# A two-layer encoder on one Trainium2 core: where the second group's FFN norm keeps its values, and which engine makes the operands of the feed-forward products

## The chip, the core and the metric

The kernel runs on one core of a Trainium2 chip. The core has a matmul engine (TensorE, PE in the profile; PEld is its weight load), three elementwise engines (VectorE or DVE, ScalarE or ACT, GpSimd or POOL) and a queue engine for transfers (SyncE, SP). ScalarE's queue issues transfers too. The metric is the time on the device of one execution, in microseconds (us); the median of three runs of the kernel before is 2719.42 us (2717.59 to 2723.7).

## The reference, cut to what matters

Two request groups ("prompt" and "sample", 512 tokens each) go through two layers with shared weights. Per layer, with `mod` a shift, scale and gate per group and channel:

```
h = rms_norm(x, norm_attn_g) * (1 + scale_a) + shift_a
x = x + gate_a * (mixers(h @ w_in) @ w_out)
h = rms_norm(x, norm_ffn_g) * (1 + scale_f) + shift_f
u = h @ w_up                                    # 1024 -> 2 x 2816
u = conv3(u, conv_w) + conv_b                   # 3 taps along the tokens, per channel
val, gate = split(u)
x = x + gate_f * ((val * silu(gate)) @ w_down)  # 2816 -> 1024
```

All of it is float32. The change touches the second half: the FFN norm, the up-projection and the down-projection.

## The kernel before

**Products in halves.** A float32 operand is used as a pair: a high half `hi` (rounded by ScalarE) and a low half `lo = value - hi`, made by an elementwise engine ("split"). One product of a 128x128 weight block with a 128x512 activation block takes three matmuls (`mm3`, L172 to L174). Tiles named `whi`, `wlo` are halves of weights, `hh`, `hl` of activations, `th`, `tl` of sums of activations. A weight split goes into a ring of 768 columns (`w_split`), so a 512-column split is one instruction or two of 256.

**Up-projection.** The 22 blocks `f` of the up-projection each have a value and a gate half. For the first `n1` = 2 blocks the four quarter products (two groups x two halves of the 1024 input channels) are computed plainly (`plain_up`, eight accumulators in all, 24 matmuls each). For the other 20 blocks seven products replace eight (the Strassen-Winograd scheme): weight blocks and activation blocks are first added and subtracted, `w_combos` for the weights, T1 to T4 for the activations, where B11, B21 are the two channel halves of group 0 and B12, B22 those of group 1. T1 = B12 - B11, T2 = B22 - T1, T3 = B22 - B12, T4 = B21 - T2, on whole values, each split again. Before, the whole values of both groups are not kept: `whole` adds `hh` and `hl` back together each time (L1091), `minus` forms the differences and the low halves (L1094). Each product of the seven (`mm7`) is 12 matmuls.

**What stands around it.** After the products of a block, ScalarE and DVE run the conv (`conv3`, L1160, L1161, L1163): ScalarE's instruction and two on DVE read the PSUM bank, so the bank is free only when L1163 is done. `glu` applies silu on ScalarE, multiplies (L1169) and stores the gate product through ScalarE's queue (L1170). The PSUM pools `p_mm`, `p_sc` and `p_tp` have two banks each. In the first layer 63 pieces of the modulation product for the second layer (`ada_cols`, L242, `csx`) are placed between the products; `ag` places eight of them after the first and the second product of block 2.

**FFN norm.** `outproj` forms the residual of a group, `norm_rstd` its per-token scale, `norm_rows` spreads the scale over the partitions with four transposes (L282), `norm_apply` scales (L296), shifts and splits. For odd channel blocks POOL makes the low half (L304), for even ones DVE (L307).

**Down-projection.** The 22 blocks are taken in groups of pairs (`gr`: 3, 3, 3 pairs and four plain blocks in layer 0; 4, 3, 4 pairs in layer 1). Per pair there are four weight sums (`w_combos`) and four activation sums (`g_combos`), seven products with a split on either side, and the results are added into the residual from PSUM (`add_x`, L1313): 28 additions per group.

**Who does what, and in which order.** Letters in the table `P` choose the engine of each elementwise step in turn ('p' POOL, 'v' DVE; 'vvp' is two of three on DVE): `uf` the first weights' splits, `tb`/`tl` the activation sums and their splits, `ug` the gate product, `us`/`ul` the later weights' sums and splits, `ds`, `db`, `dl` the down-projection's sums and splits (`d0`, `d1`, `d2` for its first group). A scheduler with a timeline of its own sets each engine's order; each engine then works its list strictly in order. `issue_after` adds an ordering between two instructions.

## Time and profile before

| | us |
|---|---|
| median of three runs | 2719.42 |
| profiled execution: device time | 2725.8 |
| profiled execution: span | 2724.0 |
| PE / DVE / ACT / POOL busy in it | 2562.2 / 2018.2 / 1410.9 / 1143.0 |

| stage | from - to | length | PE busy | DVE | POOL | clock |
|---|---|---|---|---|---|---|
| modulation, attention, output projections, layer 0 | 0 - 693.6 | 693.6 | 639.9 | 461.9 | 220.4 | 0.98 |
| plain products, layer 0 | 693.6 - 738.9 | 45.3 | 45.3 | 38.8 | 26.3 | 1.00 |
| first later products, layer 0 | 738.9 - 780.1 | 41.2 | 16.7 | 41.2 | 28.8 | 0.71 |
| other later products, layer 0 | 780.1 - 1194.3 | 414.2 | 411.4 | 302.7 | 157.4 | 1.00 |
| down-projection in pairs, layer 0 | 1194.3 - 1382.8 | 188.5 | 175.8 | 183.5 | 138.0 | 0.97 |
| rest of layer 0, attention of layer 1 | 1382.8 - 2025.2 | 642.4 | 618.8 | 408.5 | 220.4 | 0.98 |
| plain products, layer 1 | 2025.2 - 2069.7 | 44.5 | 44.5 | 38.5 | 25.3 | 1.00 |
| first later products, layer 1 | 2069.7 - 2108.6 | 38.9 | 15.9 | 38.9 | 28.4 | 0.65 |
| other later products, layer 1 | 2108.6 - 2485.1 | 376.5 | 376.4 | 300.8 | 153.2 | 1.00 |
| down-projection, layer 1 | 2485.1 - 2720.3 | 235.2 | 217.6 | 202.7 | 145.0 | 0.97 |

The page gives each engine's busy time, its course over 40 slices, and the granted clock of PE as a share of full speed. A matmul's record (0.39 us) is longer than the step to the next one, because matmuls are pipelined; the step is what counts. Idle time of PE is attributed to whatever released it: "DVE t L1163" is a conv step on DVE. A busy engine is not necessarily working at its best price, since an instruction's record also covers the time in which it is held up.

### The profile page before, as it was taken

What the parts mean: (1) busy time and instruction counts of PE and PEld (TensorE: products, weight loads), DVE (VectorE), ACT (ScalarE), POOL (GpSimd) and SP (SyncE); (2) the same over time, 40 slices, a digit from 0 to 9 for tenths busy, and PEclk for the clock granted to TensorE, in tenths of its full rate; (3) what the DMA queues carried; (4) which work ended last, traced back from release to release, by engine and by line L of the source; (5) the groups of instructions that cost most, each with busy time, mean ns of one, the idle gap of its engine ahead of it and who ended that gap; (6) DMA issues with size and microseconds to landing.
All of it is one profiled execution on the core that took longest, in us unless ns stands there. A gap on an engine that the chain in (4) does not pass through costs nothing. (4 is left out here: it accounts for less than half of the span.)

```text
span 2724.0 us, 39807 instructions
## 1 busy us (share of the span) xinstructions
PE 2562.2 (94%) x13836; PEld 2160.4 (79%) x13836; DVE 2018.2 (74%) x3639; ACT 1410.9 (52%) x3058; POOL 1143.0 (42%) x811
## 2 busy tenths in 40 slices
PE   8899999999879999998999999999996999999988
PEld 4788889888657777776788989898875888887767
DVE  6677577665887777789964765867469878878986
ACT  4466566564444445453444756756544555555422
POOL 2321212256644433428853122122667344441884
PEclk9999999999989999999999999999997999999999
DMA  7743545565144444452224345445651222224321
GB/s 265 217 116 107 130 109 141 145 188 181 66 163 144 142 140 128 151 205 101 93 76 113 86 114 136 113 118 148 191 181 47 86 78 87 76 86 185 109 85 62
DMA packets 146433, 347.69 MB, mean 128 GB/s; under 512 B 21372, under 2 KB 27260, under 8 KB 144952
## 3 DMA queue, kind: packets, MB, share of 16 engines
q1 hardware_dynamic: 133560, 322.08, 39.1%
q10 hardware_dynamic: 12672, 23.07, 2.3%
q8 instruction: 109, 1.79, 0.3%
q14 instruction: 92, 0.75, 0.1%
HBM read 241.19 MB, written 59.51 MB: 110 GB/s over the span
## 5 line engine op out<-in xcount | busy, mean ns | idle before, releaser
L162 POOL TENSOR_TENSOR wlo<-s,whi 128x768 fp32r<-128x768 f32 (+1 forms) x131 | 237.3, 1820 | 429.3 <-ACT whi L160 406.2
L172 PE MATMUL ps_mm<-hh,whi 128*128 128x512 f32 x932 | 369.7, 399 | 35.5 <-DVE t L1163 26.2
L173 PE MATMUL ps_mm<-hl,whi 128*128 128x512 f32 x932 | 369.0, 396 | 5.0 <-DVE hl L1094 3.7
L174 PE MATMUL ps_mm<-hh,wlo 128*128 128x512 f32 x932 | 367.5, 394 | 6.3 <-POOL wlo L1094 3.5
L172 PE MATMUL ps_mm<-whi,hh 128*128 128x256 f32 (+1 forms) x1104 | 342.0, 311 | 9.7 <-ACT raw L533 6.7
L173 PE MATMUL ps_mm<-wlo,hh 128*128 128x256 f32 (+1 forms) x1104 | 338.1, 307 | 1.3 <-POOL wlo L162 1.3
L174 PE MATMUL ps_mm<-whi,hl 128*128 128x256 f32 (+1 forms) x1104 | 337.9, 307 | 0.0
L1094 DVE TENSOR_TENSOR wlo<-fr,whi 128x512 fp32r<-128x512 f32 (+1 forms) x385 | 304.0, 807 | 38.2 <-ACT whi L1098 30.3
L1169 POOL TENSOR_TENSOR t<-t 128x512 f32<-128x512 f32 x88 | 127.9, 1453 | 428.0 <-issue 111.3
L1098 ACT ACTIVATE whi<-fr 128x512 fp32r<-128x512 f32 (+1 forms) x416 | 199.6, 517 | 176.3 <-PE ps_mm L173 65.5
L172 PEld LDWEIGHTS ps_mm<-hh,whi 128*128 128x128 f32 x932 | 176.2, 190 | 83.4 <-issue 22.0
L172 PEld LDWEIGHTS ps_mm<-whi,hh 128*128 128x128 f32 x1104 | 214.0, 194 | 13.4 <-ACT raw L533 7.5
L173 PEld LDWEIGHTS ps_mm<-wlo,hh 128*128 128x128 f32 x1104 | 214.3, 194 | 4.2 <-POOL wlo L162 2.2
L174 PEld LDWEIGHTS ps_mm<-whi,hl 128*128 128x128 f32 x1104 | 213.6, 194 | 1.5
L174 PEld LDWEIGHTS ps_mm<-hh,wlo 128*128 128x128 f32 x932 | 176.8, 190 | 44.1 <-POOL wlo L1094 3.9
L173 PEld LDWEIGHTS ps_mm<-hl,whi 128*128 128x128 f32 x932 | 177.0, 190 | 42.5 <-DVE hl L1094 5.4
L160 ACT ACTIVATE whi<-s 128x768 fp32r<-128x768 f32 (+1 forms) x153 | 123.6, 815 | 129.9 <-DMA s<-in_w_in 32.4
L641 DVE CUSTOM_DVE_ANT_0 S<-ps_sc,bias 128x512 f32<-128x512 f32 (+3 forms) x288 | 150.2, 529 | 53.5 <-PE ps_sc L677 41.1
L1161 DVE SCALAR_TENSOR_TENSOR t<-u,cw,t 128x511 f32<-128x511 f32 x120 | 118.1, 984 | 63.4 <-ACT t L1160 62.6
L636 DVE TENSOR_TENSOR ptl<-ps_tp,pth 128x256 fp32r<-128x256 f32 (+1 forms) x240 | 129.7, 552 | 47.8 <-ACT pth L635 46.2
L1160 ACT ACTIVATE t<-u,cw 128x512 f32<-128x512 f32 x120 | 97.6, 813 | 122.8 <-DVE u L1091 107.1
L172 PE MATMUL ps_sc<-hh,whi 128*128 128x512 f32 x404 | 159.1, 395 | 1.1 <-DVE x L1313 1.1
(351 smaller groups left out, 6934.2 us busy)
## 6 DMA issues: line engine op xcount, KB each, us to landing
fr<-in_w_up SPq DMA_DIRECT2D x88, 512.0 KB, 3.8
sa<-in_w_adac SPq DMA_DIRECT2D x56, 512.0 KB, 5.9
s<-in_w_in SPq DMA_DIRECT2D x64, 384.0 KB, 3.6
g_sp<-t ACTq DMA_DIRECT2D x88, 256.0 KB, 4.1
stk<-pr_h SPq DMA_DIRECT2D x152, 128.0 KB, 2.3
stk<-pr_l SPq DMA_DIRECT2D x152, 128.0 KB, 2.4
s<-in_w_ada SPq DMA_DIRECT2D x50, 384.0 KB, 3.3
s<-in_w_out SPq DMA_DIRECT2D x40, 384.0 KB, 3.2
```

The lines of the kernel that those rows point to most:

```text
L160: nc.scalar.activation(hi[:, :cols], s[:, :cols], AF.Copy)
L162: self.eng[self.count % len(self.eng)].tensor_tensor(lo[:, :cols], s[:, :cols], hi[:, :cols].bitcast(F32), op=ALU.subtract)
L172: nc.tensor.matmul(out_, a[0], b[0], start=start, stop=False, skip_group_check=True)
L173: nc.tensor.matmul(out_, a[0], b[1], start=False, stop=False, skip_group_check=True)
L174: return nc.tensor.matmul(out_, a[1], b[0], start=False, stop=stop, skip_group_check=True).ins
L636: nc.vector.tensor_tensor(lo[:, :n], pt[:, :n], hi[:, :n].bitcast(F32), op=ALU.subtract)
L641: nc.vector.tensor_tensor_reduce(s[:, :n], p, b, 1.0, init, op0=ALU.add, op1=ALU.min, accum_out=mn)
L1094: pick(key).tensor_tensor(o, a, b, op=ALU.subtract)
L1098: nc.scalar.activation(hi, s, AF.Copy)
L1160: nc.scalar.activation(t, p, AF.Identity, scale=c4[:, 1:2], bias=c4[:, 3:4])
L1161: nc.vector.scalar_tensor_tensor(t[:, 1:], p[:, :T - 1], c4[:, 0:1], t[:, 1:], op0=ALU.mult, op1=ALU.add)
L1169: pick('ug').tensor_tensor(a, a, b, op=ALU.mult)
```

## The change

- **Second group's norm.** `outproj` hands over the residual and the scale of group 1; the scaling, shift and split now stand in the up-projection, between the first and the second plain block of group 0. The scaled and shifted value stays whole in `xk` (first four channel blocks) and `vk`, and is split by ScalarE (high) and DVE (low). T1, T2, T3 are formed in place from the whole values, and `whole` is gone. `plain_up` takes an instruction after which its later accumulators and conv steps are issued (`x_last`, the last scaling).
- **Group 0's norm and the attention norm.** The odd-block branch with POOL is gone: ScalarE writes the high half, DVE the low half, for all blocks.
- **Engines.** A key 'ut' (= 'v') replaces 'tb', 'tl' and 'uf', and serves for the gate products of the plain blocks and the weight sums of block 2. 'ds', 'db', 'dl' become 'v' for all groups of the down-projection.
- **Modulation.** 'ag' is gone; all 63 pieces are spread from block 3.2 to block 21.2.
- **Memory.** The pool with the attention's S and residual tiles moves to the right-hand side and stays open until group 0's plain products; T1, T2 and most of T4 then take its place.

```diff
-P = {..., 'ds': 'p', 'db': 'p', 'dl': 'vvp', 'd2': 'v', ..., 'd0': 'v', 'd1': 'v', ..., 'ag': [[4, 4, 0], []]}
+P = {..., 'ds': 'v', 'db': 'v', 'dl': 'v', ..., 'ut': 'v'}
...
-                if k % 2:
-                    nc.scalar.activation(t, t, AF.Identity, bias=sh)
-                    nc.scalar.activation(hi, t, AF.Copy)
-                    norm_last[0] = nc.gpsimd.tensor_tensor(lo, t, hi.bitcast(F32), op=ALU.subtract).ins
-                else:
-                    nc.scalar.activation(hi, t, AF.Identity, bias=sh)
-                    norm_last[1] = nc.vector.scalar_tensor_tensor(lo, t, sh, hi.bitcast(F32), ...).ins
+                nc.scalar.activation(hi, t, AF.Identity, bias=sh)
+                nc.vector.scalar_tensor_tensor(lo, t, sh, hi.bitcast(F32), op0=ALU.add, op1=ALU.subtract)
...
-                    hf.append(norm_apply(s_tile, xo, norm_rows(r), l, 1, g))
+                    if g == 0:
+                        hf.append(norm_apply(s_tile, xo, norm_rows(r), l, 1, g))
+                    else:
+                        hf.append((xo, r))
...
-                    pick('ug').tensor_tensor(a, a, b, op=ALU.mult)
+                    pick('ug' if f >= NC1 else 'ut').tensor_tensor(a, a, b, op=ALU.mult)
...
-                ada_at = [NC1 + (2.5 + i) / 7 for i, n in enumerate(n_gap) for _ in range(n)]
-                rest = 9 * len(mine) - len(ada_at)
+                rest = 9 * len(mine)
...
-                    plain_up(0)
-                    with tc.issue_after(norm_last[0]), tc.issue_after(norm_last[1]):
-                        for k in range(4):
-                            u = us[k]
-                            t = ft("t")
-                            whole(t, B12[k])
-                            minus('tb', u, t, u)
-                            split('tl', u, T1[k])
...
-                    plain_up(1)
...
+                    plain_up(B11, B21, (0,))
+                    pb = norm_rows(r1)
...
+                    for k in range(KC):
+                        t = (xk + vk)[k]
+                        x_last = nc.vector.scalar_tensor_tensor(t, x1[k], ab[:, l, 1, k, 1:2], pb, op0=ALU.mult,
+                                                                op1=ALU.mult).ins
+                        nc.scalar.activation(t, t, AF.Identity, bias=mod[:, l, 3, k, 1:2])
+                        b2.append(split('ut', t, h_pair()))
+                    plain_up(B11, B21, range(1, NC1), x_last)
...
+                    for k in range(4):
+                        minus('ut', xk[k], xk[k], us[k])
+                        minus('ut', vk[k], vk[k], xk[k])
+                        split('ut', vk[k], T2[k])
+                    for k in range(4):
+                        split('ut', xk[k], T1[k])
+                    plain_up(B12, B22, range(NC1))
...
-                    qa = [w_combos('ds' if gi else 'd0', 'dl' if gi else 'd2', ...
+                    qa = [w_combos('ds', 'dl', ...
```

**Order piece 1: DVE, layer 0, around the conv of the first plain accumulator of group 1.** `t<-ps_mm,cw,t` are the two conv steps (the second one frees the bank that block 2 starts with), `th`, `tl` halves of T1, T2, T4, `sa` and `xk` whole values and differences, `wlo<-s` and `wlo<-fr` splits of weights, `fr<-s,fr` a weight sum. Before:

```order
L1161 SCALAR_TENSOR_TENSOR t<-ps_mm,cw,t 128x511
L1094 TENSOR_TENSOR t<-t,sa 128x512
L1161 SCALAR_TENSOR_TENSOR t<-ps_sc,cw,t 128x511
L1094 TENSOR_TENSOR tl_8541<-sa,th_8540 128x512
L1094 TENSOR_TENSOR wlo<-s,whi 128x256
L1094 TENSOR_TENSOR wlo<-fr,whi 128x512
L1094 TENSOR_TENSOR tl_8545<-sa,th_8544 128x512
L1163 SCALAR_TENSOR_TENSOR t<-ps_mm,cw,t 128x511
```

Now, from right behind the first conv step of that accumulator (L1157 there) to its second (L1159):

```order
L1090 TENSOR_TENSOR xk<-sa 128x512
L1090 TENSOR_TENSOR tl_8721<-sa,th_8720 128x512
L1090 TENSOR_TENSOR wlo<-s,whi 128x256
L1090 TENSOR_TENSOR fr<-s,fr 128x512
L1090 TENSOR_TENSOR xk<-sa 128x512
L1090 TENSOR_TENSOR tl_8723<-sa,th_8722 128x512
L1090 TENSOR_TENSOR xk<-sa 128x512
L1087 TENSOR_TENSOR sa<-hh,hl 128x512
L1090 TENSOR_TENSOR tl_8725<-sa,th_8724 128x512
L1157 SCALAR_TENSOR_TENSOR t<-ps_sc,cw,t 128x511
L1165 TENSOR_TENSOR t<-t 128x512
L1159 SCALAR_TENSOR_TENSOR t<-ps_mm,cw,t 128x511
```

The second conv step still stands several instructions behind the first; between them are now weight sums, differences and splits that POOL shared before, and the gate product (L1165).

**Order piece 2: POOL, same place.** `wlo<-s,whi` are splits of the output projection's weights, `t<-t` (L1169, L1165) gate products, `fr<-s,fr` weight sums. Before:

```order
L1169 TENSOR_TENSOR t<-t 128x512
L304 TENSOR_TENSOR hl<-n_t,hh 128x512 x4
L1091 TENSOR_TENSOR t<-hh,hl 128x512 x3
L1094 TENSOR_TENSOR sa<-t,sa 128x512
L1169 TENSOR_TENSOR t<-t 128x512
L1094 TENSOR_TENSOR fr<-s,fr 128x512
L1091 TENSOR_TENSOR t<-hh,hl 128x512
L1094 TENSOR_TENSOR sa<-t,sa 128x512
L1094 TENSOR_TENSOR fr<-fr 128x512 x2
L1094 TENSOR_TENSOR tl_8543<-sa,th_8542 128x512
L1094 TENSOR_TENSOR sa<-t,sa 128x512
L1094 TENSOR_TENSOR t<-t,sa 128x512
```

Now:

```order
L162 TENSOR_TENSOR wlo<-s,whi 128x768 x2
L162 TENSOR_TENSOR wlo<-s,whi 128x512
L162 TENSOR_TENSOR wlo<-s,whi 128x768
L1087 TENSOR_TENSOR s<-fr 128x512
L1090 TENSOR_TENSOR fr<-s,fr 128x512
L1090 TENSOR_TENSOR fr<-fr 128x512
L1087 TENSOR_TENSOR s<-fr 128x512
L1090 TENSOR_TENSOR fr<-fr 128x512
```

The sums, splits and gate products of the plain part have left POOL; behind the output projection's splits its next work is the weight sums of block 3.

**Order piece 3: the down-projection of layer 0, second group of pairs.** `t_` and `s_` with a number are the intermediate sums of one pair each, `hh<-hl,t` and `hl<-hl` activation sums, `sa`, `fs` weight blocks. On POOL before:

```order
L1091 TENSOR_TENSOR s_13139<-sa,fs 128x512
L1091 TENSOR_TENSOR s_13146<-sa,fs 128x512
L1091 TENSOR_TENSOR s_13155<-fs,fr 128x512
L1094 TENSOR_TENSOR t_13160<-hl,hh 128x512
L1094 TENSOR_TENSOR t_13167<-hl,hh 128x512
L1094 TENSOR_TENSOR t_13174<-hl,hh 128x512
L1094 TENSOR_TENSOR hl<-hh 128x512
L1094 TENSOR_TENSOR wlo<-sa,whi 128x256
L1094 TENSOR_TENSOR hl<-hl 128x512
L1094 TENSOR_TENSOR sa<-s_13139,sa 128x512
L1094 TENSOR_TENSOR hl<-hh 128x512
L1094 TENSOR_TENSOR hl<-hl 128x512
```

On DVE now:

```order
L1090 TENSOR_TENSOR sa<-s_13105,sa 128x512
L1090 TENSOR_TENSOR sa<-s_13112,sa 128x512
L1090 TENSOR_TENSOR fs<-s_13121,fs 128x512
L1090 TENSOR_TENSOR hh<-hl,t_13126 128x512
L1090 TENSOR_TENSOR hh<-hl,t_13133 128x512
L1090 TENSOR_TENSOR hh<-hl,t_13140 128x512
L1090 TENSOR_TENSOR hl<-hl 128x512 x3
L1316 SCALAR_TENSOR_TENSOR x_12441<-ps_tp,mod,x_12441 128x512
L1316 SCALAR_TENSOR_TENSOR x_12441<-ps_pp,mod,x_12441 128x512
L1316 SCALAR_TENSOR_TENSOR x_12441<-ps_tp,mod,x_12441 128x512
L1316 SCALAR_TENSOR_TENSOR x_12441<-ps_ov,mod,x_12441 128x512
L1090 TENSOR_TENSOR sa<-fs,sa 128x512
```

The sums of this group stood on POOL between its share of the splits; they now stand on DVE between the additions from PSUM (`x<-ps_..`).

## Rows read from the trace of the kernel before

**Rows 1.** Stages: from:to, length, busy us (count) of each engine, clock, DMA

```profile
693.60:738.90 45.30, 45.30 (x204) 37.10 (x204) 38.81 (x45) 18.97 (x32) 26.27 (x19) 1.00 0.16 57
738.90:780.10 41.20, 16.74 (x102) 11.54 (x101) 41.16 (x44) 15.66 (x28) 28.75 (x17) 0.71 0.33 117
...
1194.30:1382.80 188.50, 175.80 (x751) 141.89 (x750) 183.52 (x221) 78.11 (x155) 138.00 (x89) 0.97 0.29 102
...
2485.10:2720.30 235.20, 217.59 (x922) 175.96 (x920) 202.68 (x248) 82.99 (x166) 144.97 (x96) 0.97 0.29 100
```

**Rows 2.** PE's waits, 680 to 800 us: us in total, times, longest

```profile
PE ps_mm L172 <- DVE t L1163: 14.7, 1, 14.7
PE ps_mm L172 <- ACT u L1154: 9.8, 1, 9.8
```

**Rows 3.** PE's waits, 2030 to 2180 us

```profile
PE ps_mm L172 <- DVE t L1163: 11.6, 1, 11.6
PE ps_mm L172 <- ACT u L1154: 11.5, 1, 11.5
```

**Rows 4.** Timeline, PE behind the first wait: start, us, engine, instruction [idle before]

```profile
753.57 0.77 PE L172 MATMUL ps_mm<-hh,whi 128*128 128x512 f32 x1 [14.66 <-DVE t L1163]
...
757.82 0.39 PE L173 MATMUL ps_mm<-hl,whi 128*128 128x512 f32 x1
```

**Rows 5.** Timeline, PE in the plain products of layer 0

```profile
711.42 0.39 PE L172 MATMUL ps_sc<-hh,whi 128*128 128x512 f32 x1
...
716.86 0.39 PE L172 MATMUL ps_mm<-hh,whi 128*128 128x512 f32 x1
```

**Rows 6.** Timeline, DVE and POOL at the same time

```profile
749.35 1.75 DVE L1094 TENSOR_TENSOR wlo<-fr,whi 128x512 fp32r<-128x512 f32 x1
...
750.51 1.71 POOL L1091 TENSOR_TENSOR t<-hh,hl 128x512 f32<-128x512 f32 x1
751.02 1.75 DVE L1094 TENSOR_TENSOR tl<-sa,th 128x512 fp32r<-128x512 f32 x1
```

**Rows 7.** Timeline, DVE while POOL is idle

```profile
775.53 0.41 DVE L1094 TENSOR_TENSOR wlo<-fr,whi 128x256 fp32r<-128x256 f32 x1
...
775.87 0.68 DVE L1094 TENSOR_TENSOR t<-t 128x512 f32<-128x512 f32 x1
...
776.47 0.68 DVE L1094 TENSOR_TENSOR hl<-t,hh 128x512 fp32r<-128x512 f32 x1
```

**Rows 8.** Timeline, scale transposes and scalings of the second group

```profile
707.53 0.60 PE L282 MATMUL ps_tp<-ident,rs_y 128*128 128x128 f32 x4
...
708.24 4.70 DVE L296 SCALAR_TENSOR_TENSOR n_t<-xt,ab,ps_tp 128x512 f32<-128x512 f32 x7 [0.26 <-PE ps_tp L282]
```

**Rows 9.** PE's waits, 1220 to 1380 us

```profile
PE ps_tp L174 <- POOL wlo L1094: 7.3, 2, 7.1
PE ps_tp L172 <- DVE x L1313: 2.6, 2, 1.9
```

**Rows 10.** PE's waits, 2440 to 2724 us

```profile
PE ps_tp L174 <- POOL wlo L1094: 4.7, 2, 2.5
PE ps_mm L174 <- POOL wlo L1094: 3.5, 1, 3.5
```

**Rows 11.** DVE by form, 1255 to 1322 us: xcount, busy us, mean ns

```profile
L1094 DVE TENSOR_TENSOR hl<-hh 128x512 fp32r<-128x512 f32 x11 | 17.0, 1558 | 0.0
```

**Rows 12.** DVE by form, 1195 to 1254 us

```profile
L1094 DVE TENSOR_TENSOR hl<-hl,hh 128x512 fp32r<-128x512 f32 x6 | 3.9, 680 | 0.0
```

**Rows 13.** DVE by form, 1165 to 1197 us

```profile
L1094 DVE TENSOR_TENSOR hl<-hh 128x512 fp32r<-128x512 f32 x6 | 3.9, 682 | 0.0
...
L1094 DVE TENSOR_TENSOR t<-hl,hh 128x512 f32<-128x512 f32 x3 | 1.9, 685 | 0.0
```

**Rows 14.** Timeline, PE behind modulation pieces

```profile
780.08 0.19 PEld L172 LDWEIGHTS ps_tp<-th,whi 128*128 128x128 f32 x1 [0.41 <-PE ps_ov L242]
```

**Rows 15.** Stage of the second output projection

```profile
663.60:693.60 30.00, 28.48 (x126) 22.67 (x125) 24.78 (x28) 18.68 (x33) 24.30 (x17) 1.00 0.50 177
```

More of the change, by code (lines that the diff above doesn't have):

```diff
@@ L1080, in trunk_kernel @@
                 g_sp = g_sps[l]
-                h = hf
+                h, (x1, r1) = hf
                 engs = {'p': nc.gpsimd, 'v': nc.vector}
@@ L1249, in trunk_kernel @@
[L1249 to L1255 removed]
+                        plus('ut', us[k], B11[k][0].bitcast(F32), B11[k][1].bitcast(F32))
+                    plain_up(B11, B21, (0,))
+                    pb = norm_rows(r1)
+                    xk = [ft("xk") for k in range(4)]
@@ L1256, in trunk_kernel @@
+                    for k in range(4):
+                        plus('ut', us[k], B21[k][0].bitcast(F32), B21[k][1].bitcast(F32))
+                        minus('ut', us[k], us[k], vk[k])
+                        split('ut', us[k], T4[k])
                     for f in range(NC1, NF):
                         a, b, c = p_mm(), p_sc(), p_tp()
-                        q = w_combos('us', 'ul', up_raw(f), lambda n: W.pool.tile([128, W.width], F32, name="s", tag="s", bufs=W.stages)[:, :T])
+                        q = w_combos('us' if f > NC1 else 'ut', 'ul', up_raw(f), lambda n: W.pool.tile([128, W.width], F32, name="s", tag="s", bufs=W.stages)[:, :T])
```

67 lines of the change are left out of this document (30 added, 37 removed).

## The prediction

> **What bounds the kernel now.** I read the page's busy shares first: TensorE (PE) is busy for 94% of the span, so a change can win only where PE waits or runs slowly. The 40 slices put those places at the two up-projection starts and at the two down-projections, and the stage table [rows 1] sizes them. A 128x512 product costs 0.227 us at full clock: 24 of them pass between the two rows of [rows 5], 5.44 us. The start of the later products in layer 0 (from 738.9 us) holds two waits, 14.7 and 9.8 us [rows 2], and after each wait products come at 0.43 us: the ten after the first take 4.25 us instead of 2.27 [rows 4], and the twelve after the second lose 12 x 0.20 = 2.4 by the same step. The granted clock of that stage is 0.71 [rows 1]: part of those products ran at the lower of PE's two levels, 1.2 GHz, behind a wait in which PE did nothing. Loss there: 14.7 + 9.8 + 2.0 + 2.4 = 28.9 us. Layer 1 repeats it with 11.6 and 11.5 us [rows 3] and again 4.4 us of slow products: 27.5 us.
>
> The down-projections take 188.5 and 235.2 us [rows 1]. The code issues 3 x 252 = 756 and 11 x 84 = 924 products there, 171.4 and 209.5 us at full pace. Loss: 17.1 and 25.7 us. All four places together: 99.2 us.
>
> What PE waits for is the next question. The releasers are VectorE (DVE) and POOL: at the starts a conv step on DVE (L1163) that frees a PSUM bank, and a copy that stands behind it [rows 2, 3]; in the down stages mostly low halves made by POOL [rows 9, 10]. Both engines are late for one reason. While POOL runs a two-input elementwise instruction, DVE's own takes 1.75 us and one starts every 1.67 us, and POOL's takes 1.71 [rows 6]; alone, DVE starts one every 0.60 us at 0.68 us each [rows 7]. In the time in which the pair finishes two, DVE alone would finish 2.8. The same split averages 1558 ns in the down stage beside a busy POOL [rows 11] and 680 ns in the group before it, where DVE makes nearly all operands [rows 12]. DVE's 97% busy share of the layer 0 down stage [rows 1] is mostly this stretching.
>
> **The change part by part.** Prices: a two-input instruction on DVE 0.60 us, a 256-column piece 0.34 [rows 7], one with a PSUM input 0.66 (seven in 4.70 us, the last one 0.74 long [rows 8]).
>
> *Start of the up-projection.* Removed per layer: 16 re-additions of high and low halves (24 before, 8 now), since the second group's whole values stay in xk and vk. Moved from POOL to DVE: the first weights' splits, the remaining sums and splits, four gate products, the four weight sums of block 2. POOL's list then goes from the last output-projection split straight to block 3's sums (second order piece), so DVE's price here is 0.60, not 1.7. I laid the new DVE list along PE's eight plain groups of 24 products (5.44 us each; the fifth starts at 716.9 [rows 5], the eighth ends at 738.9 [rows 1]). The scale transposes, at 707.5 us now [rows 8], move to the end of the second group, two groups and themselves before 716.9, so 705.3; scales are ready at 705.9. Eight scalings and one conv step, 9 x 0.66 = 5.9 us, end at 711.8. "Scaling ahead of conv" thus costs the second conv step up to 6 us, for which nobody waits: that bank is next used at 722. The first four low halves come six instructions later, 715.5, ahead of 716.9; the last of the eight by 722.4, where PE wants it at 721.5: 1 us. From 705.9 to the conv step that frees the bank of the first later product stand 52 instructions, 31.9 us: 737.8, and PE arrives at 738.9 plus that 1 us. In time, where it was 14.7 us late. The second bank's step comes 12 instructions later (7.1 us), at 744.9, wanted at 742.6: 2.3 us. One more wait follows: before the fifth product the accumulator is copied out by ScalarE, behind a gate function and a conv step that need DVE's next 11 us; I get 757.4 where PE arrives at 753.1, 4.3 us. With 1 us of slow products that is 8.6, taken as 9 us left of 28.9, and 9 of 27.5 in layer 1, whose lists read alike. Gain 19.9 + 18.5 = 38.4.
>
> *Ahead of it.* The first weights' splits (eight halves in ten pieces, 5.0 us) and four low halves of the first group now stand on DVE during the second output projection, where DVE is busy 24.8 of 30 us beside a POOL that still splits output weights [rows 15] and where DVE adds each output bank. I charge 2 us per layer for banks freed late, with bounds 0 (the idle 5.2 us absorb it) and 7 us (all lands on PE): cost 4.
>
> *Modulation pieces.* Eight of the 63 matmul pieces leave the first later block; four of them stood inside the second wait, hidden. Their PE time stays in the total; four more interruptions at about 0.4 us idle each [rows 14] cost 1.6 us. The SP queue issues their loads later, into the buffers of us and vk, free some ten microseconds before their first use.
>
> *Cover for the rest.* ScalarE's queue carries the stores of the gate products, which now wait for DVE instead of POOL; behind them stand copies and conv steps. By the list above DVE passes each product before ScalarE needs its next input, except the one charged as 4.3 us. The new buffers on the right-hand side wait for the attention's last reads, done when the scalings are (712 us). In layer 1 the loads of block 2's weights lose two spare buffers and start when the first splits are done, more than 15 us before their first reader. These cost nothing.
>
> *Down-projections.* Groups 2 and 3 lose POOL altogether (third order piece). DVE's work per group of three chunk pairs: 24 sums, 21 + 14 full-width splits, 14 pieces of 256, 28 additions from PSUM: 59 x 0.60 + 14 x 0.34 + 28 x 0.66 = 58.6 us against PE's 57.1. For four pairs: 72.1 against 76.2. Layer 1 (4, 3, 4): DVE 202.8, PE 209.5, so DVE stays ahead and I leave 2 us of boundary waits per group: 6 of 25.7, gain 19.7. Layer 0 (3, 3, 3): DVE 175.8 against 171.4. It starts about ten instructions ahead, 6 us (nine of them in [rows 13]), and has 5.3 us of additions behind the last operand. That leaves it 2.6 us late there, 1.9 for the first operands of the plain rest, and I add 1.2 per group at boundaries: 8 of 17.1, gain 9.1.
>
> A rule of the Trainium skill speaks against this part: Perfetto Trace Analysis, Optimizing Scalar/DVE Operations, advises taking work off a saturated DVE. It adds that between DVE and GpSimd this may not help, since they share a read port. By the first half the down stages lengthen (the fourth rival); the trace sides with the second half, 1.75 against 0.68 us.
>
> *Sum*: 38.4 - 4 - 1.6 + 9.1 + 19.7 = 61.6 us. The profiled execution took 2725.8 us (span 2724.0), 6.4 us above the median of 2719.4; 61.6 off the median gives 2657.8.
>
> **The rivals.** *DVE becomes the bound of the down stages*: its order leaves it idle at times, and what it then lacks it cannot make up at 58.6 against 57.1. For: the two numbers are within 3%. Against: layer 1 has 7 us of slack. Without both down gains 38.4 - 5.6 = 33 us are left, 2687; with the starts at only two thirds, 2699.
>
> *The new waits do not appear*: 9 us per start shrink to 3, the 14 us of the down stages to 3: 61.6 + 12 + 11 = 84.6 us, 2635. For: they come from a hand-laid list with every instruction at full price.
>
> *Slower, by order*: DVE obeys its list in order, and an addition that frees a PSUM bank stands behind splits whose input is not there yet. There are 42 product boundaries in the down stages. If each loses 1.5 us more than granted, 63 us, the gain is gone; at a batch of four splits each (2.4 us) the time is 2658 + 101 = 2759. Against: layer 0's first group had DVE nearly alone already, and waits on DVE in that stage are 2.6 us in all [rows 9].
>
> *Slower, wrong price*: the 1.56 us is not POOL's doing but belongs to these operands. Then POOL's 89 and 96 instructions of the down stages [rows 1] bring DVE 139 and 150 us more, with 5 and 32 us free: about +250 us, over 2900. This is what the first half of the rule quoted from Perfetto Trace Analysis would do. Against: same shape, both prices within 25 us [rows 6, 7].
>
> **How the numbers follow.** Forecast as summed 0.55 (2640 to 2675); DVE-bound down stages 0.20 (2675 to 2700); fewer waits 0.15 (2615 to 2640); nothing gained that can be measured 0.03; slower 0.06 by order and 0.01 by price. The range, 2630 to 2698, takes in the forecast with its bounds, nearly all of the DVE-bound case and half of the good one. About 0.2% is what a measurement of this kernel can tell from no change; by these cases faster 0.90, same 0.03, slower 0.07.
>
> **What would show it.** Right: at the two starts no PE wait above 5 us and a clock near 1.00; POOL nearly empty in the down stages; DVE's split there at 680 ns; down stages near 180 and 216 us. DVE-bound: PE waiting in many small pieces for DVE's wlo and hl through all groups of layer 0. Wrong price: DVE's splits above 1 us with POOL idle. A PE wait at the fifth plain group would show that the second group's norm comes too late. Equal gaps at the starts with short DVE instructions would refute the whole step.

## The result and the profile after

| | before | changed |
|---|---|---|
| median, us (runs) | 2719.18 (4) | 2668.89 (4) |
| ratio, 95% interval | 1 | 0.9817 [0.9802, 0.9832] |
| profiled execution: device time / span | 2725.8 / 2724.0 | 2666.95 / 2665.2 |
| PE / DVE / ACT / POOL busy in it | 2562.2 / 2018.2 / 1410.9 / 1143.0 | 2546.1 / 1990.3 / 1408.2 / 735.9 |

The change saves 50.3 us; 61.6 were forecast (2657.8 us). Timed a second time, beside the kernel before, the ratio was 0.9809 [0.9790, 0.9829].

To compare stages between kernels I divide each trace at the same products: every kernel here issues 13,374 matmuls without the modulation pieces, and a stage runs from the end of one such product (start of its record plus 0.227 us) to the end of another. The products chosen lie up to three off the true change of stage. It matters in one place: the boundaries behind the output projections lie one product (layer 0) and three products (layer 1) late, so the wait in front of the first plain product counts to the output projection. Where that matters below, I also give the times with exact boundaries.

| stage, us | before | changed | again | down-projection alone | combined |
|---|---|---|---|---|---|
| up to the second output projection, layer 0 | 664.1 | 660.0 | 662.2 | 659.2 | 659.5 |
| second output projection, layer 0 | 29.6 | 34.1 | 34.3 | 29.6 | 31.2 |
| plain products, layer 0 | 45.0 | 47.5 | 47.5 | 45.0 | 45.8 |
| later products, layer 0 | 455.6 | 436.3 | 439.1 | 455.3 | 434.9 |
| down-projection in pairs, layer 0 | 188.5 | 174.0 | 174.1 | 179.5 | 181.1 |
| its plain rest | 34.7 | 39.9 | 39.7 | 34.7 | 34.7 |
| attention of layer 1 | 577.8 | 580.4 | 580.3 | 575.5 | 577.5 |
| second output projection, layer 1 | 29.7 | 32.2 | 32.2 | 30.3 | 31.9 |
| plain products, layer 1 | 44.5 | 45.0 | 45.0 | 44.5 | 45.6 |
| later products, layer 1 | 415.6 | 398.6 | 399.7 | 415.2 | 397.6 |
| down-projection, layer 1 | 235.0 | 212.8 | 212.6 | 212.6 | 212.9 |

("Again" is the changed kernel in a second profile; the last two columns are experiments below. "Combined" is the changed kernel with three small edits.)

The stage view of the changed kernel, where [rows 1] and [rows 15] stood (from:to, length, then busy us and count of PE, PEld, DVE, ACT, POOL, the granted clock, DMA share, GB/s): output projection and plain products of layer 0, its down-projection and plain rest, the down-projection of layer 1.

```profile
660.00:694.10 34.10, 28.66 (x122) 22.16 (x121) 28.80 (x41) 16.11 (x28) 6.94 (x4) 1.00 0.43 142
694.10:741.60 47.50, 46.98 (x205) 38.35 (x204) 39.44 (x69) 27.56 (x48) 1.28 (x1) 0.96 0.10 35
...
1177.90:1351.90 174.00, 171.23 (x752) 140.43 (x751) 174.00 (x299) 77.60 (x154) 10.09 (x3) 1.00 0.35 125
1351.90:1391.80 39.90, 37.00 (x161) 29.42 (x160) 18.80 (x27) 8.45 (x15) 16.04 (x11) 0.96 0.20 76
...
2448.00:2660.80 212.80, 210.66 (x922) 173.65 (x920) 200.20 (x342) 83.85 (x166) 2.88 (x2) 0.99 0.31 110
```

POOL went from 138.0 to 10.1 us and from 145.0 to 2.9 us in the down stages, as forecast. In layer 0 DVE is now busy for all of the 174.0 us, in layer 1 for 200.2 of 212.8. The first two lines are where the change costs something: 34.1 us where it was 29.6, and a clock of 0.96 behind it. With the boundary exactly behind the last product of the output projection, this stage goes from 28.2 to 31.4 us in layer 0 and from 28.3 to 31.4 in layer 1, and the plain products with the wait in front of them go from 46.4 to 50.1 in layer 0 and from 45.8 to 45.7 in layer 1. So about 3.1 us are lost inside the output projection of each layer, and 3.7 us behind it in layer 0 alone.

PE's waits in the changed kernel (us in total, times, longest): 640 to 735 us, then the start of the later products in layer 0 and in layer 1. They answer to [rows 2, 3].

```profile
PE ps_mm L172 <- DVE xt L1003: 6.5, 7, 2.3
PE ps_mm L173 <- DVE hl L1090: 0.5, 1, 0.5
```

```profile
PE ps_mm L172 <- ACT u L1150: 4.6, 1, 4.6
PE ps_sc L172 <- DVE t L1159: 2.6, 1, 2.6
```

```profile
PE ps_mm L172 <- ACT u L1150: 7.2, 1, 7.2
PE ps_sc L172 <- DVE t L1159: 2.4, 1, 2.4
```

The waits of 14.7, 9.8, 11.6 and 11.5 us have given way to these. The lists gave 2.3 us for the second bank and 4.3 for the fifth product; they are 2.6 and 4.6 in layer 0, 2.4 and 7.2 in layer 1. The wait for a low half of the second group, forecast at 1 us, is 0.5.

DVE by form in the second group of the down-projection, layer 0 (xcount, busy us, mean ns), where [rows 11] had 1558 ns:

```profile
L1090 DVE TENSOR_TENSOR hl<-hh 128x512 fp32r<-128x512 f32 x15 | 9.9, 677 | 0.0
...
L1316 DVE SCALAR_TENSOR_TENSOR x<-ps_tp,mod,x 128x512 f32<-128x512 f32 x7 | 5.2, 738 | 0.0
...
L1090 DVE TENSOR_TENSOR wlo<-fs,whi 128x256 fp32r<-128x256 f32 x6 | 2.5, 412 | 0.0
```

A split takes 677 ns with POOL idle: the fourth rival, by which the high price belonged to the operands, is out. The Trainium skill (Perfetto Trace Analysis, Optimizing Scalar/DVE Operations) says that offloading a saturated DVE may make sense, but that between DVE and GpSimd it might not help; these rows side with the second half. The third rival, an addition or split stuck in DVE's list at each of the 42 boundaries, is out too: PE's waits in the pairs of layer 0 are few:

```profile
PE ps_mm L173 <- DVE hl L1090: 1.5, 2, 0.9
PE ps_tp L173 <- DVE hl L1090: 1.2, 1, 1.2
```

Three places show what is left or new. First, the output projection in layer 0 and its end (timeline: start, us, engine, instruction [idle before, and what ended it]):

```profile
671.05 1.77 DVE L300 SCALAR_TENSOR_TENSOR hl<-n_t,mod,hh 128x512 fp32r<-128x512 f32 x1
...
673.64 0.47 PE L172 MATMUL ps_mm<-hh,whi 128*128 128x512 f32 x1 [1.37 <-DVE xt L1003]
...
688.56 0.69 DVE L1090 TENSOR_TENSOR wlo<-fr,whi 128x512 fp32r<-128x512 f32 x1
...
689.76 0.75 DVE L1003 SCALAR_TENSOR_TENSOR xt<-ps_mm,mod,xt 128x512 f32<-128x512 f32 x1
...
690.56 0.50 PE L172 MATMUL ps_mm<-hh,whi 128*128 128x512 f32 x1 [0.90 <-DVE xt L1003]
...
692.29 0.69 DVE L1087 TENSOR_TENSOR s<-fr 128x512 f32<-128x512 f32 x1 [1.79 <-DMA fr<-in_w_up]
692.90 0.74 DVE L1003 SCALAR_TENSOR_TENSOR xt<-ps_mm,mod,xt 128x512 f32<-128x512 f32 x1
...
693.79 0.47 PE L172 MATMUL ps_mm<-hh,whi 128*128 128x512 f32 x1 [2.27 <-DVE xt L1003]
```

The lines down to 690.56 show work that DVE got with the change: low halves of the first group (L300, one of them 1.77 us long beside POOL's splits of output weights) and splits of the first up-projection weights (`wlo<-fr`) stand in front of additions (L1003) that free PSUM banks. Measured from product to product, PE loses 1.5 us more than before at 673.6, and 1.4 us more in three waits from 687 to 691. Layer 1 shows the same steps. Behind that, in layer 0 alone, DVE stands idle for 1.79 us in front of the first weight sum of block 2 (L1087, `s<-fr`), whose weights are still on their way; behind it in DVE's list stands the addition that frees a PSUM bank, and PE waits 2.27 us for that, where the longest wait before was 1.0. Eight of its next steps take 0.43 us instead of 0.227: 1.6 us.

Second, the start in layer 1:

```profile
2062.25 2.20 POOL L1090 TENSOR_TENSOR fr<-s,fr 128x512 f32<-128x512 f32 x1 [46.22 <-issue]
...
2063.91 4.44 DVE L1090 TENSOR_TENSOR t4l<-sa,t4h 128x512 fp32r<-128x512 f32 x3
...
2070.33 0.79 PE L172 MATMUL ps_mm<-hh,whi 128*128 128x512 f32 x1 [7.19 <-ACT u L1150]
```

The three low halves of T4 take 4.44 us together, 1.48 each, because the weight sums of block 3 have begun on POOL; the copy that ends PE's 7.19 us comes behind them.

Third, the boundary between the pairs and the plain rest in layer 0:

```profile
1351.11 5.21 POOL L162 TENSOR_TENSOR wlo<-s,whi 128x768 fp32r<-128x768 f32 x2 [154.16 <-DMA hl<-g_sp]
...
1353.00 1.64 DVE L1090 TENSOR_TENSOR hl<-hh 128x512 fp32r<-128x512 f32 x1
...
1354.57 0.74 DVE L1316 SCALAR_TENSOR_TENSOR x<-ps_sc,mod,x 128x512 f32<-128x512 f32 x1
1355.23 1.65 DVE L1090 TENSOR_TENSOR hl<-hl,hh 128x512 fp32r<-128x512 f32 x1
...
1355.45 0.47 PE L172 MATMUL ps_sc<-hh,whi 128*128 128x512 f32 x1 [2.80 <-DVE x L1316]
```

POOL begins the next layer's weight splits (L162), and DVE's splits beside them take 1.64 and 1.65 us. The additions that read PSUM, in between, keep their 0.74.

### The profile page after: what moved, and what is told of

It reads as the page before. It is cut to its first block, busy times and chain, and to the rows that moved or that the text cites. A ratio compares the mean times of both kernels' runs of the same rounds, so it can differ in the third digit from the quotient of the medians.

```text
span 2665.2 us, 39593 instructions
## 1 busy us (share of the span) xinstructions
PE 2546.1 (96%) x13836; PEld 2149.7 (81%) x13836; DVE 1990.3 (75%) x3881; ACT 1408.2 (53%) x3050; POOL 735.9 (28%) x537
## 3 DMA queue, kind: packets, MB, share of 16 engines
q8 instruction: 109, 1.79, 0.3%
## 4 chain that ended last, share of the span: by engine, by line
PE 68%; DVE 15%; DMA 7%; issue 5%; ACT 3%; SPq 1%; POOL 1%; ACTq 0%; DVEq 0%; POOLq 0%
PE ps_mm L172 13%; PE ps_mm L173 13%; PE ps_mm L174 13%; PE ps_tp L172 3%; PE ps_tp L173 3%; PE ps_tp L174 3%; PE ps_sc L172 3%; PE ps_sc L174 3%; PE ps_sc L173 3%; DVE hl L1090 2%; DMA s<-in_w_ada 2%; DVE wlo L1090 2%; DVE x L1316 2%; DMA s<-in_w_in 1%; PE ps_ov L242 1%
## 5 line engine op out<-in xcount | busy, mean ns | idle before, releaser
L162 POOL TENSOR_TENSOR wlo<-s,whi 128x768 fp32r<-128x768 f32 (+1 forms) x131 | 238.9, 1832 | 604.8 <-ACT whi L160 424.7
L1090 DVE TENSOR_TENSOR wlo<-fr,whi 128x512 fp32r<-128x512 f32 (+1 forms) x416 | 293.2, 724 | 43.3 <-ACT whi L1094 39.3
L1165 POOL TENSOR_TENSOR t<-t 128x512 f32<-128x512 f32 x80 | 117.3, 1466 | 398.3 <-DVE t L1159 158.8
L629 DVE TENSOR_TENSOR ptl<-ps_tp,pth 128x256 fp32r<-128x256 f32 (+1 forms) x240 | 130.1, 550 | 47.0 <-ACT pth L628 45.6
L1157 DVE SCALAR_TENSOR_TENSOR t<-u,cw,t 128x511 f32<-128x511 f32 x120 | 117.2, 977 | 63.2 <-ACT t L1156 62.6
```

The costliest lines, as they stand in the source:

```text
L162: self.eng[self.count % len(self.eng)].tensor_tensor(lo[:, :cols], s[:, :cols], hi[:, :cols].bitcast(F32), op=ALU.subtract)
L629: nc.vector.tensor_tensor(lo[:, :n], pt[:, :n], hi[:, :n].bitcast(F32), op=ALU.subtract)
L1090: pick(key).tensor_tensor(o, a, b, op=ALU.subtract)
L1157: nc.vector.scalar_tensor_tensor(t[:, 1:], p[:, :T - 1], c4[:, 0:1], t[:, 1:], op0=ALU.mult, op1=ALU.add)
L1165: pick('ug' if f >= NC1 else 'ut').tensor_tensor(a, a, b, op=ALU.mult)
```

## Experiments

Each ratio is to the kernel before, timed in the same set. There are three sets: the first four experiments; the next four; and the last four, with the changed kernel among them.

| kernel | median, us | ratio | 95% interval |
|---|---|---|---|
| changed | 2668.89 | 0.9817 | 0.9802 - 0.9832 |
| before, down-projection on DVE | 2687.81 | 0.9874 | 0.9855 - 0.9893 |
| changed, down-projection shared | 2703.21 | 0.9926 | 0.9903 - 0.9950 |
| changed, a third of the plain part on POOL | 2684.82 | 0.9857 | 0.9837 - 0.9877 |
| changed, block 2's sums on POOL | 2666.18 | 0.9790 | 0.9771 - 0.9810 |
| changed, block 3's sums held | 2677.88 | 0.9829 | 0.9809 - 0.9849 |
| changed, next layer's splits held | 2667.73 | 0.9792 | 0.9776 - 0.9809 |
| changed, attention norm as before | 2668.63 | 0.9797 | 0.9782 - 0.9812 |
| changed, first splits on POOL | 2664.36 | 0.9782 | 0.9767 - 0.9797 |
| changed again | 2671.14 | 0.9809 | 0.9790 - 0.9829 |
| changed, first splits and block 2's sums on POOL | 2662.03 | 0.9778 | 0.9760 - 0.9797 |
| changed, block 3's sums on DVE | 2672.29 | 0.9811 | 0.9792 - 0.9830 |
| combined | 2658.84 | 0.9769 | 0.9752 - 0.9786 |

**The down-projection alone, and everything but it.**

```diff
# kernel before, in P (...: the other keys stay)
...
-'ds': 'p', 'db': 'p', 'dl': 'vvp'
+'ds': 'v', 'db': 'v', 'dl': 'v'
...
# changed kernel: the same keys back, with 'd0', 'd1', 'd2' for the first group
```

> The kernel before with one part of the change alone: all sums and splits of the down-projection on DVE. Theory (the stretched price of 1.56 us comes from POOL running at the same time): the down stages go from 188.5 and 235.2 us to about 174 and 213 us, the plain rest of layer 0 loses some 5 us as in the changed kernel, together 31 us: 2688 us (2690 by the prediction's own terms of 9.1 and 19.7 us). DVE splits there at 0.68 us. The starts of the up-projection keep their waits of 14.7, 9.8, 11.6 and 11.5 us. Rival (the price belongs to these operands, or the gain of the down stages needs the earlier start that the other parts give): 2719 us or more.

> The changed kernel with the down-projection's sums and splits shared with POOL as before. Theory: the other half of the same comparison, 2669 + 31 = 2700 us, down stages back near 188 and 235 us with DVE splits near 1.56 us, starts as in the changed kernel (waits of 2.6 and 4.6, 2.4 and 7.2 us). If the two parts are independent, the gain of the first kernel of this call and the loss of this one are equal within 5 us. Rival (they need one another): one of the two is far smaller than the other.

Stages and PE's waits at the two starts, down-projection alone:

```profile
1189.10:1368.70 179.60, 173.17 (x752) 141.61 (x752) 179.47 (x307) 78.64 (x155) 11.84 (x3) 0.99 0.31 107
2468.70:2681.40 212.70, 210.76 (x922) 173.85 (x920) 200.06 (x341) 83.84 (x166) 2.87 (x2) 0.99 0.32 110
```

```profile
PE ps_mm L172 <- DVE t L1163: 14.7, 1, 14.7
PE ps_mm L172 <- ACT u L1154: 9.6, 1, 9.6
```

```profile
PE ps_mm L172 <- DVE t L1163: 11.6, 1, 11.6
PE ps_mm L172 <- ACT u L1154: 11.0, 1, 11.0
```

DVE by form in the second group of layer 0, changed kernel with the shared down-projection:

```profile
L1090 DVE TENSOR_TENSOR hl<-hh 128x512 fp32r<-128x512 f32 x12 | 18.7, 1564 | 0.0
...
L1316 DVE SCALAR_TENSOR_TENSOR x<-ps_tp,mod,x 128x512 f32<-128x512 f32 x8 | 5.9, 737 | 0.0
...
L1090 DVE TENSOR_TENSOR wlo<-fs,whi 128x256 fp32r<-128x256 f32 x4 | 4.9, 1240 | 0.0
```

The theory held on both sides. With the down-projection alone the stages take 179.5 + 34.7 us in layer 0 (before: 188.5 + 34.7) and 212.6 in layer 1 (235.0), while the waits at the starts stay at 14.7, 9.6, 11.6 and 11.0. With the sharing put back they take 190.8 + 34.7 and 234.2, and the split goes from 677 to 1564 ns, while the starts keep the changed kernel's waits (2.6 and 4.6, 2.4 and 5.6 us). This part is worth 1.3% (the one ratio), the rest of the change 0.7% (the other): 2.0 together, measured 1.8 to 1.9, so the two add within the intervals. The loss of 5.2 us in the plain rest of the changed kernel is no separate cost either: where the rest keeps its 34.7, the pairs take 179.5 instead of 174.0. In both kernels PE loses some 5 us once in the third group of pairs or at its end: in this one to a low half that comes 3.3 us late some 35 us ahead of the boundary, in the changed kernel to an addition at the boundary, each time with slow products behind the wait. The order decides where the lateness shows.

**Fewer instructions, or no neighbour?**

```diff
-'ut': 'v'
+'ut': 'vvp'
```

> The changed kernel with every third of the plain part's sums, splits and gate products on POOL: the re-additions stay away, only the engine changes back for a third. Theory (contention): some 22 instructions per layer on POOL at 1.7 us; beside each DVE finishes one at 1.67 us where it could finish 2.8, so DVE comes about 8 us later to the conv steps of each layer, and with slow products behind the waits the kernel loses about 20 us: 2689 us, DVE's instructions beside POOL at 1.7 us. Rival (it is the number of instructions: 16 fewer re-additions per layer): 2669 us or less, since DVE has fewer to do.

Stages of layer 0 (output projection, plain products) and PE's waits in the plain products:

```profile
662.40:697.10 34.70, 28.67 (x122) 22.21 (x121) 29.34 (x38) 15.82 (x29) 12.45 (x8) 1.00 0.38 125
697.10:749.30 52.20, 47.37 (x204) 38.13 (x204) 45.55 (x55) 25.61 (x45) 25.02 (x17) 0.93 0.11 37
```

```profile
PE ps_mm L173 <- DVE hl L1090: 4.8, 2, 4.2
```

It loses 0.4%, about 11 us, half of what I expected, and in another place. The plain products take 52.2 and 52.1 us (47.5 and 45.0 in the changed kernel), because low halves of the second group come late (4.8 us of waits in layer 0), and layer 1's output projection 37.3 (32.2); the later products are no slower at all, 434.9 and 393.6 (436.3, 398.6), since DVE has less left to do there. So a neighbour on POOL costs time where DVE's results are due at once, and keeping POOL out is part of the gain; but the waits at the starts did not grow with a third of the plain part on POOL (1.7 and 2.0 us, and a new one of 1.6, in layer 0). The rival, by which only the number of instructions counts, gives no loss and is out. How the gain at the starts divides between POOL's absence, the 16 re-additions saved and the new order is not settled by this or any other run.

**The cost ahead of the starts.** Two kernels relieve DVE during the output projection:

```diff
-q = w_combos('us' if f > NC1 else 'ut', 'ul', ...
+q = w_combos('us', 'ul', ...
# the other kernel
-first[f] = [w_split('ut', s, ...
+first[f] = [w_split('uf', s, ...
```

> The changed kernel with the four weight sums of block 2 on POOL. Reason: in the trace of the changed kernel the first of these sums stands in DVE's list ahead of an addition that frees a PSUM bank of the output projection, and waits 1.8 us there for its weights; PE waits 2.3 us and its next products run at half pace. Theory: that wait goes (4 us in layer 0, 1 in layer 1) and DVE's list at the start of the later products is four instructions shorter (2.4 us per layer), so 2659 us. Rival (the sums on POOL stretch DVE's work beside them as much as they relieve it): 2666 to 2669 us.

> The changed kernel with the splits of the first up-projection weights on POOL, as before. Theory (the prediction charged these splits on DVE with 2 us per layer in the output projection; the trace shows 4.4 and 2.5 us): the stage of the second output projection goes from 34.1 and 32.2 us back to some 31 and 30 us, the first plain products keep full pace: 2664 us. Rival (POOL's splits stretch DVE's additions and the start of the plain part by as much): 2669 us.

The output projection and plain products of layer 0, first with block 2's sums on POOL, then with the first splits there:

```profile
659.30:690.90 31.60, 28.44 (x122) 22.19 (x121) 28.08 (x40) 15.12 (x26) 7.49 (x4) 1.00 0.40 123
690.90:736.70 45.80, 45.28 (x204) 36.89 (x203) 40.14 (x65) 29.26 (x52) 11.24 (x5) 1.00 0.14 52
```

```profile
662.80:694.00 31.20, 28.30 (x122) 22.12 (x121) 25.36 (x33) 16.56 (x29) 16.64 (x12) 1.00 0.42 138
694.00:739.90 45.90, 45.38 (x204) 37.14 (x204) 39.67 (x67) 27.70 (x48) 3.12 (x3) 1.00 0.15 56
```

Together 77.4 and 77.1 us, where the changed kernel has 81.6: the wait of 2.3 us and the slow products behind it are gone in both (clock 1.00 in both lines). In the second kernel the sum stays on DVE, but the shorter list puts it behind the last additions. The totals are alike, the places are not. With exact boundaries, block 2's sums on POOL leave the output projection at 31.4 us and bring the plain products from 50.1 to 46.0; the first splits on POOL bring the output projection to 29.9 and the plain products to 47.2, with a wait of 1.0 us left in front of them. So the late-fed sum cost some 4 us in layer 0, and the splits on DVE 1.5 us inside the output projection. What is left there, 29.9 against 28.2 us, is the wait behind the first group's low halves, which all kernels with the changed norm show and which no run took out by itself. In layer 1, where no sum stood in the way, block 2's sums on POOL bring nothing (31.4 us); the first splits on POOL bring the same 1.5 us (29.9), but 1.2 us come back as a wait in front of the plain products (46.9, changed 45.7). The other gain that I expected, shorter starts with block 2's sums on POOL, did not come: 436.5 and 398.5 us.

**Block 3's sums.** Held on POOL until DVE has made the low halves of T4, and, in another kernel, made by DVE:

```diff
+gate[0] = nc.gpsimd.tensor_copy(row_tile(), T4[3][1][:, :256].bitcast(F32)).ins
... # block 3's sums and differences are issued after gate[0]
# the other kernel
-q = w_combos('us' if f > NC1 else 'ut', ...
+q = w_combos('us' if f > NC1 + 1 else 'ut', ...
```

> The changed kernel with a small copy on POOL ahead of the weight sums of block 3, which reads the last low half of T4 and so holds these sums until DVE has made it. Reason: in the trace of the changed kernel the last PE wait of each start (4.6 and 7.2 us) ends with a copy behind DVE's low halves of T4, and two or three of these take 1.4 to 1.6 us each beside the first sums on POOL. Theory (contention is what is left of the wait): they fall to 0.65 us, the wait shrinks by some 2 us in layer 0 and 3 in layer 1, and slow products behind it by one: 2663 us. Rival (the sums of block 3 then come too late, and PE waits for them instead): 2669 us or more.

> The changed kernel with the weight sums of block 3 on DVE too, so that POOL starts a block later. Holding these sums back on POOL made the kernel slower, since the products then waited for the sums. Theory (contention is what stretches the last wait of each start): DVE's low halves of T4 fall from 1.4 to 1.6 us to 0.65, the four sums cost 4 x 0.6 = 2.4 us per layer: about even in layer 0, 2 us gained in layer 1, 2 us in all. Rival (DVE is the bound of the start, and its number of instructions decides): the last waits grow by 2.4 us per layer, 5 us slower.

Held: DVE, ScalarE and PE in layer 0's start (timeline).

```profile
753.26 1.27 DVE L1097 TENSOR_TENSOR t4l<-sa,t4h 128x512 fp32r<-128x512 f32 x2
753.43 0.63 ACT L1171 ACTIVATE t<-t 128x512 f32<-128x512 f32 x1 [2.23 <-DVE t L1166]
...
753.97 0.58 ACT L1157 ACTIVATE u<-ps_mm 128x512 f32<-128x512 f32 x1
...
754.60 0.79 PE L172 MATMUL ps_mm<-th,whi 128*128 128x512 f32 x1 [6.78 <-ACT u L1157]
...
761.78 0.42 ACT L1101 ACTIVATE whi<-fr 128x256 fp32r<-128x256 f32 x1 [3.99 <-POOL fr L1097]
```

On DVE: low halves of T4 and PE's waits in layer 0, then PE's waits in layer 1.

```profile
762.30 1.30 DVE L1090 TENSOR_TENSOR t4l<-sa,t4h 128x512 fp32r<-128x512 f32 x2
```

```profile
PE ps_mm L172 <- ACT u L1150: 3.1, 1, 3.1
PE ps_sc L172 <- DVE t L1159: 2.6, 1, 2.6
```

```profile
PE ps_sc L172 <- DVE t L1159: 2.4, 1, 2.4
PE ps_mm L172 <- DVE u L1087: 2.3, 1, 2.3
PE ps_mm L172 <- ACT u L1150: 1.9, 1, 1.9
```

In both kernels two low halves take 1.27 to 1.30 us where they took 2.80: the stretching is gone. Held, nothing is gained. The copy `u` of the first accumulator (753.97), which ran at 744.57 in the changed kernel, now stands behind a gate function in ScalarE's list, and PE waits 6.78 us for it; and ScalarE waits 3.99 us for the late sums (761.78). The first of these is a change of order that came with the edit, so this run doesn't test the theory cleanly. With the sums on DVE the last wait falls from 4.6 to 3.1 us in layer 0, and from 7.2 to 1.9 in layer 1 with a new one of 2.3 behind it; but DVE's four extra instructions lengthen the plain products by 1.0 and 0.6 us, and the kernel's ratio, 0.9811, is that of the changed one in the same set, 0.9809. Stretching beside POOL is thus shown to be a part of these waits, but taking it away this way gains nothing, since DVE's own list gets longer.

**The next layer's splits.**

```diff
+W.hold = nc.gpsimd.tensor_copy(td("t1")[:, :256], gl[-1][1][1][:, :256].bitcast(F32)).ins
... # POOL's weight splits are issued after W.hold
```

> The changed kernel with a small copy on POOL ahead of layer 1's first two weight splits, which reads the last low half of layer 0's down-projection and so holds these splits until DVE has made it; nothing else in the order changes. Reason: in the trace of the changed kernel the two splits run from 1351.1 to 1356.3 us, DVE's splits beside them take 1.64 us, and PE waits 2.8 us and runs slowly behind that. Theory: the plain rest of layer 0 falls from 39.9 to some 35 us, 2664 us. Rival (the additions and splits come late by DVE's own order): 39.9 us stay, 2669 us.

PE's waits from 1352 to 1393 us with the splits held:

```profile
PE ps_sc L173 <- DVE x L1317: 2.4, 2, 1.8
```

The plain rest takes 37.7 us, between 39.9 and the 35 that I expected; DVE's splits are at 0.68 us again, and PE still waits 1.8 us for an addition that stands behind others in DVE's list. So about 2.2 us of the 5.2 were POOL's doing; the 3.0 that stay I put down to DVE's order, which no run changed alone. The ratio, 0.9792, does not stand clear of the changed kernel's.

**The attention norm.**

```diff
+if j == 0 and k % 2:   # attention norm only
... # POOL's branch for odd blocks, as before
```

> The changed kernel with POOL's low halves of odd channel blocks put back in layer 1's attention norm alone. Reason: the stage from that norm to layer 1's second output projection takes 580.4 us where it took 577.8. Theory (PE waits for low halves that now all come from DVE): the stage returns to some 577.5 us, 2666 us. Rival (the difference is what this stage varies by from run to run): no change, 2669 us.

The stage takes 578.9 us. Kernels that share the changed norm had 576.6 to 581.0, two that have it as before 577.8 and 575.5. A cost of some 2 us is possible; these runs don't settle it.

**The changed kernel again, and combinations.**

> The changed kernel itself, beside the three below on the same chip, so that differences of a few microseconds can be read. Theory: the ratio to the kernel before is 0.98 again, the stages repeat within 1 us except the first 660 us and the attention of layer 1, which have varied by some 5 us between kernels that leave them alone.

> The changed kernel with both the splits of the first up-projection weights and the four weight sums of block 2 on POOL. Each alone brought the output projection and plain part of layer 0 from 81.6 to 77.3 us. Theory (DVE's list there is freed for the additions that release PSUM banks; what is left of the two is independent): some 76 us in layer 0, 1 us less in layer 1, the later products as with block 2's sums alone: 6 us under the changed kernel of this call. Rival (POOL now works beside DVE through the whole plain part, and the scalings or low halves of the second group come late): PE waits in the plain part, no gain.

> The changed kernel with the first up-projection weights' splits on POOL, block 3's sums on DVE and layer 1's first weight splits held back by a small copy. Theory (they act in different places and add): 4.4 + 2 + 2 = 8 us under the changed kernel of this call. Rival (block 3's sums on DVE cost as much as the rest brings): within 2 us of the changed kernel with the first splits on POOL alone, which stood 4 to 5 us under it.

The first 660 us, which the change doesn't touch, took 657.3 to 665.4 us in these kernels, and the later products of layer 0 differ by 2.8 us between two profiles of one kernel. With both the first splits and block 2's sums on POOL the stages ahead of the starts take 77.1 us, as with either, and with exact boundaries they divide as with the first splits alone (29.9 and 47.2 us): once those are off DVE, moving the sums brings nothing more. The ratio 0.9778 is that of the first splits alone (0.9782). The combination (first splits on POOL, block 3's sums on DVE, next layer's splits held) is the fastest kernel: 2658.84 us, 12.3 below the changed one in its set, with an interval that lies below that of the changed kernel's first timing and just below that of its second. PE's waits at its start of layer 1 are 2.5, 2.4 and 1.9 us, where the changed kernel had 7.2 and 2.4.

Against the second profile of the changed kernel its output projection and plain products of layer 0 are 4.8 us shorter (77.0, 81.8) and the later products 4.2 and 2.1; the down-projection of layer 0 with its rest is 2.0 longer (215.8, 213.8). That is 9 us; against the first profile, by the same stages, 5. The rest of the 12 lies in stages that none of the three edits touches. Nor is it shown that the other two edits add to the first: the first splits alone stand at 0.9782 [0.9767, 0.9797] against 0.9769 [0.9752, 0.9786], and the stages from the second output projection to the end of the down-projection, both layers together, add up to the same in both profiles, 1415.4 and 1415.6 us. That is what the rival said, by which block 3's sums on DVE cost as much as the rest brings.

## Why the prediction was right or wrong

| term | forecast | by stages, changed | again |
|---|---|---|---|
| start, layer 0 with modulation pieces (19.9 - 1.6) | +18.3 | +19.3 | +16.5 |
| start, layer 1 | +18.5 | +17.0 | +15.9 |
| ahead of the starts, both layers | -4.0 | -10.0 | -10.2 |
| down-projection, layer 0 with its rest | +9.1 | +9.3 | +9.4 |
| down-projection, layer 1 | +19.7 | +22.2 | +22.4 |
| sum | 61.6 | 57.8 | 54.0 |

**The mechanism was right.** POOL's neighbourhood was what stretched DVE. In the down stages two runs show it, one that takes POOL out of the kernel before and one that puts it back: with POOL gone the price is the solo one, and the stages fall to 174.0 and 212.8 us, for which 180 and 216 were forecast. At the starts the waits shrank about as summed, but what part of that is POOL's absence is not separated. The list that was laid out instruction by instruction gave the new waits at the start of layer 0 to 0.3 us, though with one part by luck: the sum priced every instruction at 0.60 us to the end of the start, and left out that POOL is at work again by then, on block 3. The last low halves cost 1.4 to 1.5 us each. With these sums on DVE the last wait is 3.1 us in layer 0 and, in two pieces, 4.2 in layer 1: by this difference 1.5 and 3.0 us of the 4.6 and 7.2 are stretching. That is also more than half of why layer 1, for which I took layer 0's 9 us because "the lists read alike", has the longer wait.

One of the signs named for being right did not come in full. At the starts there was to be no PE wait above 5 us and a clock near 1.00; layer 1 has a wait of 7.2 us, and the granted clock is 0.95 over the first 31.2 us in layer 0 and 0.89 over the first 30.5 us in layer 1, where 0.71 and 0.65 stood. And one reading was wrong: the view of [rows 9] holds 1.1 and 0.7 us of further waits on DVE, so "2.6 us in all" should be 4.4. The argument against the third rival was weaker by that, though the rival did not come.

**The step that was off** is the charge of 2 us per layer for the output projection, 4 in all. It was 7 us in layer 0 and 3 in layer 1, by two causes. The work that I had charged cost more than I gave it: with exact boundaries, each layer's output projection grew by 3.1 us, half of it behind the first group's low halves and half behind the first weights' splits, 6.3 us in place of 4. DVE's idle 5.2 us did not absorb it, because the added instructions stand in front of additions that free banks. And one cause was left out: in layer 0 a weight sum that waits for its load stands in front of such an addition, and with the slow products behind that wait the plain products lost 3.7 us. Under "cover for the rest" I followed the late loads of layer 1 only; the moved sums of block 2 were counted as four instructions of 0.60 us and not asked when their data arrive. The upper bound of 7 us per layer just holds.

**Layer 0's down stage** came as summed, and by the reason given: DVE has 100% there, is the bound by a few us, and makes PE lose 5 us once, in the third group or at its end. (How the sum came to 2.6 us of lateness there can't be redone from the numbers beside it.) The second rival, DVE as the bound of the down stages, is true of this stage, and yet the 9 us came; layer 1 has the slack that the sum gave it.

**"Scaling ahead of conv"** does nothing: without its ordering the program comes out the same, in the order of every engine and in what each instruction waits for. The 6 us for which "nobody waits" belong to the order in which DVE's list was written anyway.

**The rest of the difference.** By stages the change gives 54 to 58 us, by medians 50. The profiled execution of before lay 6.6 us above its median and that of the changed kernel 1.9 below: 8.6 of the 11.1 us between forecast and median. I had seen the 6.4 and taken the loss of the profiled execution off the median in full. The stages that the change leaves alone vary by several us between executions, as the first line of the stage table shows, so what part of the 99 us of losses a median run has is not known.

## What to carry to other kernels

Before moving work between DVE and POOL, compare the price of one instruction alone and beside the other engine; where the pair finishes less than the one alone, the offload is worth something only while the results aren't due. For each instruction that is moved into a list, ask two things: how long it takes, and when its input arrives, because everything behind it in the list waits with it. Here the first cost 3.1 us per layer, since the additions behind were due at once, and the second 3.7 us in one place. When a stage table is made from counted products, check on which side of a boundary a wait falls: mine put both costs into one stage. And when the gain is read from one profiled execution, make the forecast of a median with the scatter of the untouched stages in mind.

## What the runs showed of the hardware

Beside a busy POOL, DVE's two-input instructions with all operands in SBUF took 1564 ns instead of 677 (512 columns) and 1240 instead of 412 (256 columns), while in the same stretch the ones that read PSUM kept their 737 to 738 ns. The two groups are also different operations (TENSOR_TENSOR and SCALAR_TENSOR_TENSOR), but that is not the reason. In the changed kernel SCALAR_TENSOR_TENSOR with all operands in SBUF took 1.77 us beside POOL (671.05, shown above), and over the whole kernel before, the 65 of that kind that ran their first 0.6 us beside a POOL instruction took 1631 ns on average, against 749 alone; the 53 TENSOR_TENSOR that read PSUM beside POOL took 700, against 707 alone. I had not expected so clean a division: DVE's additions from PSUM ran beside POOL at full pace, its splits did not.
